# A two-layer decoder trunk on one core: running sums of its own for a shared term of the down product, and other buffers and a priority at the start of the MLP

## The chip, the cores and the metric

The kernel runs on one core of a Trainium2 chip. The metric is the device time of one execution in microseconds (us); lower is better. The engines that matter are TensorE (PE: matmuls, and PEld: its weight loads), VectorE (DVE), ScalarE (ACT), GpSimd (POOL) and SyncE (SP), which here only issues DMAs. Each engine works through its own queue strictly in order: an instruction that waits holds back all that stand behind it.

## The reference, cut to what matters

The trunk has two layers on an activation of 1024 positions by 1024 channels, all float32. Layer 0 mixes tokens with a gated MLP, layer 1 with dilated attention. After each mixer comes the part that the change is about, a dense MLP with squared ReLU:

```python
h = x
for layer in range(DEPTH):                       # DEPTH = 2
    y = _rms_norm(h, mix_norm_g[layer])
    h = h + mixer(y)                             # gMLP, then dilated attention
    y = _rms_norm(h, mlp_norm_g[layer])
    h = h + jnp.square(jax.nn.relu(y @ w_up[layer])) @ w_down[layer]
return _rms_norm(h, final_norm_g)                # D_MODEL 1024, D_FF 4096
```

## The kernel before, in words

**Number format.** Every float32 operand is split into a high and a low part (`split`, L201: ScalarE writes the high part with a copy, L202; VectorE subtracts to get the low part, L203), and every product is three matmul passes (`three`, L327). A tile is 128 partitions by 512 columns; h lies on the chip as eight tiles `h[0..7]` of 128 channels by 1024 positions. `half(s)` is one half of the positions.

**Order.** Only TensorE's order is written out by hand. On the other engines the tile framework orders the instructions ahead of time, by its own estimate of when each will be ready; among instructions that are ready, the one earlier in the program goes first, and `tc.high_priority(offset=PRIO)` moves a group forward by 60 places in that ranking. Buffers come from pools with a fixed number of tiles: `temp()` takes one of eight tiles "t", `spare()` one of two tiles "b", `raw()` one of four tiles "r" (the landing place of weights), `wpair()` one of eight split weight pairs "wp", `pair()` one of 28 larger slots. PSUM has three banks "mm" and five banks "at". Who asks for a tile that is taken waits until its last reader is done.

**The MLP's start** (`mlp`, L647, and `Terms.second`, L402). The up product first runs plainly for two column blocks q = 0 and 1 of the hidden layer. For s = 0, then s = 1, eight groups of twelve matmuls run over four banks; at the end of each s the four banks are evacuated by `squared` (L628: ScalarE Relu from PSUM, L630, and Square in place, L631) into four `temp()` tiles c. With s = 0 three of the banks are mm and one is at; with s = 1 two are at and two are mm, so TensorE needs two mm banks back early in s = 1. While s = 0 runs, `second` makes the normalised input for s = 1: for each k in 0 to 3 two tiles t (L411 and L412, a `temp()` each), their splits, two sums in spares (L416, L417) and two sums on GpSimd (L418, L419). After s = 0 the weights of q = 2 are loaded into raw tiles (`up_weights(2)`, L673).

**The rest of the up product.** For q = 2 to 15 a two-by-two blocking is computed with seven products instead of eight (Winograd's variant of Strassen's scheme); the hidden terms of every q go to DRAM (`hid`).

**The down product** (`Down`, L735). Eighteen steps t = 0 to 17; step t works on the output rows a = t mod 4 and a + 4, and on up to four hidden blocks ks, so the four values of a take turns and each comes four or five times. A full step has seven products of twelve matmuls, in this order: d from w5, b from w6, a_ from w1, e from w7, then d further with w3, a_ further with w2, e further with w4. In between, for the next step: four raw loads of weights and their sums on GpSimd (L357 to L362), seven splits "wp" (`more()`), seven loads t<-hid (`self.inputs`) and their splits "hx". Each product's result is added by VectorE into one of the four blocks `hs[i, s]` of h (`add`, L785, L786). The sum u = b + a_ (M6 + M1) is common to three of the four blocks. Before, every step forms it anew: ScalarE copies a_ to a temp (L803), VectorE adds b (L804), GpSimd adds u to `hs[1,1]`, `hs[1,0]` and `hs[0,1]` (L816, L817). As `a_` takes the w2 product on top, TensorE cannot start it before a_ has been read for u; d with w3 likewise waits until `add(1, 1, d)` (L793) has read d. After the last step `close` (L837) multiplies hidden block 15 in and hands h on to the next norm.

The weights are loaded one step ahead, and the raw tile of a weight is free again when its split is done; SyncE's queue holds the weight loads and the loads t<-hid in one line.

Of the kernel before, what the change touches and what calls it, by code (L numbers as in the profile page):

```python
# [12 lines left out]
AF = mybir.ActivationFunctionType  # L13
# [98 lines left out]
def trunk(ctx: ExitStack, tc: tile.TileContext, xT, w_u, w_v, w_o, w_s, b_s, w_qkv, w_bo, rel,  # L112
# [14 lines left out]
    def temp():  # L127
        return tpool.tile([P, HALF], F32, tag="t", name="t")

    def spare():  # L130
        return tpool.tile([P, HALF], F32, tag="b", name="b", bufs=2)
# [8 lines left out]
    class Pair:  # L140


        def __init__(self, t):
            self.hi, self.lo = t[:, 0, :], t[:, 1, :]
# [15 lines left out]
    def raw():  # L160
        return tpool.tile([P, HALF], F32, tag="r", name="r", bufs=4)
# [218 lines left out]
    class Terms:  # L380
# [21 lines left out]
        def second(self, sq, gi):  # L402
            r = sq.rms()
            yield LAT["rms"]
            pb = spread(r)
            tt = nc.vector.tensor_tensor
            for k in range(4):
                y, x, (y0, y1) = [], [], (self.kept[k][:, j, :] for j in range(2))
                for j in range(2):
                    o = 4 * j + k  # L410
                    t = temp()  # L411
                    nc.vector.scalar_tensor_tensor(t, h[o][:, sq.cols], vec[:, gi, o:o + 1], pb, op0=ALU.mult, op1=ALU.mult)  # L412
                    y.append(t)
                    x.append(pair().split(t))
                t1, t2 = spare(), spare()
                tt(t1, y[0], y0, op=ALU.subtract)  # L416
                tt(t2, y[1], t1, op=ALU.subtract)  # L417
                nc.gpsimd.tensor_tensor(y0, y[1], y[0], op=ALU.subtract)  # L418
                nc.gpsimd.tensor_tensor(y1, y1, t2, op=ALU.subtract)  # L419
                yield 2 * LAT["tile"]  # L420
                for j in range(2):
                    self.blocks[j, 1].append(x[j])
                self.t[5].append(pair("t1").split(t1))
                self.t[6].append(pair("t2").split(t2))
# [203 lines left out]
    def squared(t, src=None):  # L628

        nc.scalar.activation(t, t if src is None else src, AF.Relu)  # L630
        nc.scalar.activation(t, t, AF.Square)  # L631
# [15 lines left out]
    def mlp(layer, x, first, last):  # L647


        def up_weights(q):  # L650
            return Weights(lambda i, j: w_up[layer, q, i, j])


        tiles = [(q, i) for q in range(2) for i in range(2)]
        c = {}
        for s in range(2):
            banks = [at_bank() if (n < 2) == (s == 1) else mm_bank() for n in range(4)]
            if s == 0:
                banks = [mm_bank() if n < 3 else at_bank() for n in range(4)]
            order = [(j, k) for j in range(2) for k in range(4)] if s == 0 else [(j, k) for k in range(4) for j in range(2)]  # L660
            for n, (j, k) in enumerate(order):
                xs = x.blocks[j, s]
                flow.until(lambda: len(xs) > k)
                for b, (q, i) in zip(banks, tiles):
                    three(b, first[q][i, j], blk(k), xs[k], n == 0, n == 7)
                    flow.pump()
            for b, (q, i) in zip(banks, tiles):
                c[q, i, s] = temp()
                squared(c[q, i, s], b)
                if s and i:  # L670
                    hidden_terms(q, c[q, 0, 0], c[q, 1, 0], c[q, 0, 1], c[q, 1, 1], c[q, 0, 0])
            if s == 0:
                w = up_weights(2)  # L673
                for _ in w.steps():
                    pass
        x.rest()

        for q in range(2, 16):
            down = Down(layer) if q == 15 else None
            wn = down.weights(0) if down else up_weights(q + 1)  # L680
            more = ahead(wn)
            more()
            d = at_bank()
            product(d, w[5], x.t[5])
            more()
            c22 = temp()
            nc.scalar.activation(c22, d, AF.Copy)  # L687
            if down:
                down.take(14, held, SEVEN[:4])
            b = at_bank()  # L690
            product(b, w[6], x.t[6])
            more()
            if down:
                down.take(14, held, SEVEN[4:])
            a = mm_bank()
            product(a, w[1], x.t[1])
            more()
            u = temp()
            nc.scalar.activation(u, a, AF.Copy)
            nc.vector.tensor_tensor(u, u, b, op=ALU.add)  # L700
            if down:
                down.early(SEVEN[:4])
            e = at_bank()
            product(e, w[7], x.t[7])
            more()
            nc.vector.tensor_tensor(c22, c22, e, op=ALU.add)  # L706
            nc.vector.tensor_tensor(c22, c22, u, op=ALU.add)
            squared(c22)
            if down:
                down.early(SEVEN[4:])  # L710
            product(d, w[3], x.t[3], True)
            more()
            c12 = temp()
            nc.vector.tensor_tensor(c12, u, d, op=ALU.add)
            squared(c12)
            product(a, w[2], x.t[2], True)
            more()
            c11 = temp()
            squared(c11, a)
            product(e, w[4], x.t[4], True)  # L720
            more()
            c21 = temp()
            nc.vector.tensor_tensor(c21, u, e, op=ALU.add)
            squared(c21)
            if q < 14:
                hidden_terms(q, c11, c21, c12, c22, u)
            elif q == 14:
                held = hidden_terms(q, c11, c21, c12, c22, u, False)
            else:
                kept(q, {(0, 0): c11, (1, 0): c21, (0, 1): c12, (1, 1): c22})  # L730
            w = wn
        down.run(w)
        down.close(last)

    class Down:  # L735


        def __init__(self, layer):
            self.layer = layer
            self.order = [14, *range(14)]  # L740
            self.x = {k: {} for k in self.order}
            self.todo = [(t % 4, range(max(0, t - 3), min(t, 14) + 1)) for t in range(18)]

        def weights(self, t, **kw):
# [28 lines left out]
        def run(self, w):  # L773
            for t, (a, ks) in enumerate(self.todo):
                hs = {(i, s): h[a + 4 * i][:, half(s)] for i in range(2) for s in range(2)}
                wn = None
                if t < 17:
                    wn = self.weights(t + 1, **(dict(own=temp, place=pair) if t == 16 else {}))
                more = ahead(wn)
                more()  # L780

                def xs(p):
                    return [self.x[self.order[k]][p] for k in ks]

                def add(i, s, src, engine=nc.vector):  # L785
                    engine.tensor_tensor(hs[i, s], hs[i, s], src, op=ALU.add)  # L786

                if t == 16:
                    self.ends(0)
                d = at_bank()  # L790
                product(d, w[5], xs(5))
                more()
                add(1, 1, d)  # L793
                self.inputs(t + 1, (5,))
                b = at_bank()
                product(b, w[6], xs(6))
                more()
                self.inputs(t + 1, (6,))
                a_ = mm_bank()
                product(a_, w[1], xs(1))  # L800
                more()
                u = temp()
                nc.scalar.activation(u, a_, AF.Copy)  # L803
                nc.vector.tensor_tensor(u, u, b, op=ALU.add)  # L804
                self.inputs(t + 1, (1,))
                if t == 16:
                    self.ends(1)
                e = at_bank()
                product(e, w[7], xs(7))
                more()  # L810
                add(1, 1, e)
                self.inputs(t + 1, (7,))
                product(d, w[3], xs(3), True)
                more()
                add(0, 1, d)
                for i, s in ((1, 1), (1, 0), (0, 1)):  # L816
                    add(i, s, u, nc.gpsimd)  # L817
                self.inputs(t + 1, (3,))
                product(a_, w[2], xs(2), True)
                more()  # L820
                add(0, 0, a_)
                self.inputs(t + 1, (2,))
                product(e, w[4], xs(4), True)
                more()
                add(1, 0, e)
                self.inputs(t + 1, (4,))
                w = wn

# [554 lines left out]
```

## Time and profile before

| | |
|---|---|
| device time, median of three runs | 2249.78 us (2249.32 to 2254.13) |
| the profiled execution: its own time | 2249.28 us |
| the profiled execution: its span, first to last instruction | 2247.6 us |
| PE busy | 2165.0 us, 96% of the span |
| DVE, ACT, POOL busy | 1605.8, 1096.9 and 636.3 us |
| mean granted TensorE clock | 0.989 |
| matmuls and transposes | 10378 |

The up product with q = 2 and on is at about 340 to 625 us and 1610 to 1898 us, the down product at about 627 to 942 us and 1898 to 2209 us, the attention between the two layers. Where PE never waits, it starts about 222 matmuls in 50 us. A stretch with fewer is a stretch with waits, and only there can the time come down, since the change takes away no matmul. In a row of the timeline stand the start, the duration, the engine, the line, the operation, output<-inputs, the count, and in brackets the idle time before it with what ended it. In the view of waits stand the engine and line that waited, what they waited for, the sum in us, how often, and the longest.

### The profile page before, as it was taken

To read this page: it belongs to the slowest core of one execution; us is meant where nothing else is said; L and a number is where in the kernel's file an instruction comes from. 1 tells how busy PE (TensorE), PEld (TensorE's weight loads), DVE (VectorE), ACT (ScalarE), POOL (GpSimd) and SP (SyncE) were. 2 spreads that over 40 slices of the span, in tenths; PEclk is the share of its full clock that TensorE was granted. 3 is DMA by queue.
4 is the path that set the end of the run, shared out by engine and by line. 5 is a ranking of instruction groups with operands and counts; after the bars stand their busy time and mean duration, and the time that the engine had idled before them with its cause. 6 is when DMAs were issued, how large, how long until landed. Compare 5 with 4: busy or idle time off the path is not lost. (4 is left out here: it accounts for less than half of the span.)

```text
span 2247.6 us, 30296 instructions
## 1 busy us (share of the span) xinstructions
PE 2165.0 (96%) x10378; PEld 1782.2 (79%) x10378; DVE 1605.8 (71%) x2823; ACT 1096.9 (49%) x2253; POOL 636.3 (28%) x456
## 2 busy tenths in 40 slices
PE   8999999999989999999999999999899999999997
PEld 6888877888877777778888888887678888777786
DVE  6875277767798888765664755647887777987877
ACT  6644145555554343456544555646455556444333
POOL 1100223333255555510000000002333333655554
PEclk9999999999999999999999999999999999999998
DMA  6321114444354444301111111120154443444433
GB/s 220 108 76 47 38 41 146 155 155 150 119 167 141 139 138 141 108 30 39 43 40 43 34 40 48 31 52 11 38 182 151 155 155 127 159 141 150 133 102 103
DMA packets 152334, 230.27 MB, mean 102 GB/s; under 512 B 32761, under 2 KB 47220, under 8 KB 152180
## 3 DMA queue, kind: packets, MB, share of 16 engines
q1 hardware_dynamic: 151280, 227.11, 31.5%
q8 instruction: 81, 1.33, 0.2%
q10 hardware_dynamic: 900, 1.23, 0.2%
q14 instruction: 73, 0.60, 0.1%
HBM read 170.45 MB, written 57.84 MB: 102 GB/s over the span
## 5 line engine op out<-in xcount | busy, mean ns | idle before, releaser
L179 PE MATMUL mm<-y,whi 128*128 128x512 f32 x1616 | 508.2, 396 | 1.0 <-DVE h L300 1.0
L179 PE MATMUL at<-hx,wp 128*128 128x512 f32 x1770 | 423.2, 394 | 30.0 <-DVE h L786 25.3
L179 PEld LDWEIGHTS at<-hx,wp 128*128 128x128 f32 x1770 | 333.1, 190 | 109.6 <-ACT wp L202 28.6
L203 DVE TENSOR_TENSOR wp<-r,wp 128x512 fp32r<-128x512 f32 (+3 forms) x388 | 331.3, 862 | 87.7 <-ACT wp L202 86.3
L179 PEld LDWEIGHTS mm<-y,whi 128*128 128x128 f32 x1616 | 296.5, 188 | 62.7 <-DVE h L300 1.4
L202 ACT ACTIVATE wp<-r 128x512 fp32r<-128x512 f32 (+3 forms) x388 | 227.6, 594 | 225.1 <-PE at L179 100.1
L256 POOL TENSOR_TENSOR t<-t 128x512 f32<-128x512 f32 (+1 forms) x66 | 82.7, 1253 | 874.1 <-ACT t L251 862.1
L179 PE MATMUL mm<-y,wlo 128*128 128x512 f32 x808 | 315.8, 391 | 0.0
L179 PE MATMUL at<-t,wp 128*128 128x512 f32 x1344 | 314.4, 390 | 0.1
L179 PEld LDWEIGHTS at<-t,wp 128*128 128x128 f32 x1344 | 252.2, 188 | 53.1 <-DVE t L706 0.9
L202 ACT ACTIVATE hx<-t 128x512 fp32r<-128x512 f32 x192 | 119.1, 626 | 271.0 <-DMA t<-hid 267.5
L203 DVE TENSOR_TENSOR hx<-t,hx 128x512 fp32r<-128x512 f32 x192 | 193.4, 1012 | 73.9 <-ACT hx L202 73.1
L179 PE MATMUL mm<-y,wp 128*128 128x512 f32 x912 | 225.9, 394 | 9.7 <-ACT t L630 9.3
L179 PEld LDWEIGHTS mm<-y,wp 128*128 128x128 f32 x912 | 171.9, 189 | 48.0 <-ACT t L630 10.8
L786 POOL TENSOR_TENSOR h<-h,t 128x512 f32<-128x512 f32 x108 | 164.0, 1535 | 157.7 <-DVE h L786 90.8
L357 POOL TENSOR_TENSOR t<-r 128x512 f32<-128x512 f32 (+3 forms) x62 | 92.4, 1490 | 353.7 <-DMA r<-in_w_up 193.4
L179 PEld LDWEIGHTS mm<-y,wlo 128*128 128x128 f32 x808 | 151.7, 188 | 33.1
L179 PE MATMUL mm<-hx,wp 128*128 128x512 f32 x708 | 172.4, 391 | 4.8 <-ACT t L803 4.8
L203 DVE TENSOR_TENSOR wlo<-r,whi 128x512 fp32r<-128x512 f32 x160 | 111.5, 719 | 74.6 <-ACT whi L202 74.5
L179 PEld LDWEIGHTS mm<-hx,wp 128*128 128x128 f32 x708 | 132.5, 188 | 34.6 <-ACT t L803 7.4
L202 ACT ACTIVATE whi<-r 128x512 fp32r<-128x512 f32 x160 | 97.2, 627 | 116.9 <-PE mm L179 91.2
L179 PE MATMUL at<-y,wp 128*128 128x512 f32 x480 | 120.6, 394 | 3.7 <-ACT t L687 3.0
(191 smaller groups left out, 3117.5 us busy)
## 6 DMA issues: line engine op xcount, KB each, us to landing
t<-hid SPq DMA_DIRECT2D x182, 256.0 KB, 4.0
hid<-t SPq DMA_DIRECT2D x140, 256.0 KB, 2.3
r<-in_w_up SPq DMA_DIRECT2D x128, 256.0 KB, 2.7
r<-in_w_dn SPq DMA_DIRECT2D x88, 256.0 KB, 2.7
r<-in_w_qkv SPq DMA_DIRECT2D x72, 256.0 KB, 2.8
hid<-b SPq DMA_DIRECT2D x56, 256.0 KB, 2.3
r<-in_w_v SPq DMA_DIRECT2D x48, 256.0 KB, 3.5
h<-in_xT SPq DMA_DIRECT2D x16, 256.0 KB, 6.1
```

Of the source, the lines that this page charges most:

```text
L179: nc.tensor.matmul(out, lhsT, rhs, **kw)
L202: nc.scalar.activation(hi, src, AF.Copy)
L203: nc.vector.tensor_tensor(lo, src, hi.bitcast(F32), op=ALU.subtract)
L256: nc.gpsimd.tensor_tensor(self.acc, self.acc, sq, op=ALU.add)
L357: tt(r3, r[0, 0], r[1, 0], op=ALU.subtract)
L786: engine.tensor_tensor(hs[i, s], hs[i, s], src, op=ALU.add)
```

## The change

It has three parts. First, `Terms.second` takes its tiles t from the raw pool instead of the temp pool. Second, the evacuations of the first two column blocks (`squared` after s = 0 and s = 1) get a priority. Third, the down product keeps one sum u per output row group a, `self.u[a]`, over all steps: u[0] and u[1] lie in the two spares, u[2] and u[3] in two temps. In steps 0 to 3 ScalarE copies b into it; from step 4 on VectorE adds b; in every step VectorE adds a_. Only in steps 14 to 17, the last for each a, does GpSimd add it to the three blocks of h; the add to `hs[1, 0]` comes after the add of e.

```diff
@@ Terms.second
-                    t = temp()
+                    t = raw()
@@ mlp
                 c[q, i, s] = temp()
-                squared(c[q, i, s], b)
+                with tc.high_priority(offset=PRIO):
+                    squared(c[q, i, s], b)
@@ Down.__init__
+            self.u = {}
@@ Down.run
                 b = at_bank()
                 product(b, w[6], xs(6))
                 more()
+                if t < 4:
+                    self.u[a] = spare() if t < 2 else temp()
+                    nc.scalar.activation(self.u[a], b, AF.Copy)
+                else:
+                    nc.vector.tensor_tensor(self.u[a], self.u[a], b, op=ALU.add)
                 self.inputs(t + 1, (6,))
                 a_ = mm_bank()
                 product(a_, w[1], xs(1))
                 more()
-                u = temp()
-                nc.scalar.activation(u, a_, AF.Copy)
-                nc.vector.tensor_tensor(u, u, b, op=ALU.add)
+                nc.vector.tensor_tensor(self.u[a], self.u[a], a_, op=ALU.add)
...
                 add(0, 1, d)
-                for i, s in ((1, 1), (1, 0), (0, 1)):
-                    add(i, s, u, nc.gpsimd)
+                if t >= 14:
+                    for i, s in ((1, 1), (0, 1)):
+                        add(i, s, self.u[a], nc.gpsimd)
...
                 add(1, 0, e)
+                if t >= 14:
+                    add(1, 0, self.u[a], nc.gpsimd)
```

## The prediction

> **What bounds the kernel now.** I read the page first (PE busy 96%), then the windows, to see where PE runs short of its own pace, and last who it waits for there.
>
> ```profile
> 400.00:450.00 50.00, 50.00 (x222) 41.41 (x221) 36.70 (x42) 24.82 (x43) 17.34 (x12) 1.00 0.45 156
> 640.00:900.00 260.00, 243.79 (x1050) 197.84 (x1049) 223.84 (x262) 109.07 (x198) 140.51 (x94) 0.99 0.43 142
> 1920.00:2160.00 240.00, 229.58 (x996) 186.26 (x995) 201.44 (x240) 98.43 (x178) 131.11 (x84) 1.00 0.44 144
> 1600.00:1610.00 10.00, 4.14 (x12) 2.67 (x11) 9.89 (x14) 6.27 (x12) 4.43 (x4) 0.72 0.07 26
> ```
>
> The columns are the stretch, its length, busy time and count of PE, PEld, DVE, ACT, POOL, then clock and DMA. The up product (first row) starts 222 matmuls in 50 us, 0.225 us each. At that pace the 1050 and 996 matmuls of the two down stretches would take 236 and 224 us: about 24 and 16 us are lost there. In the ten microseconds of the last row, the MLP's start in layer 1, 12 matmuls start instead of 44. The up product has nothing to give. The waits name the holders:
>
> ```profile
> PE at L179 <- DVE h L786: 27.1, 24, 3.4
> PE mm L179 <- ACT t L630: 9.3, 2, 5.9
> PE mm L179 <- ACT t L803: 4.8, 6, 1.3
> ```
>
> The first and third rows are the down product (adds into h; the copy of a_), the second the MLP's start, once per layer. All three together are 41 us of waiting. The change takes no matmul away, so this is its ceiling.
>
> **The MLP's start.** The timeline of layer 1:
>
> ```profile
> 1598.77 2.20 PE L179 MATMUL at<-y,wp 128*128 128x512 f32 x9
> 1605.68 0.61 ACT L202 ACTIVATE y<-t 128x512 fp32r<-128x512 f32 x1
> 1606.20 0.58 ACT L630 ACTIVATE t<-mm 128x512 f32<-128x512 f32 x1
> 1606.83 3.17 PE L179 MATMUL mm<-y,wp 128*128 128x512 f32 x6 [5.86 <-ACT t L630]
> 333.36 0.63 ACT L202 ACTIVATE y<-t 128x512 fp32r<-128x512 f32 x1 [1.70 <-DVE t L412]
> 333.90 1.06 ACT L630 ACTIVATE t<-mm 128x512 f32<-128x512 f32 x2
> 334.53 2.78 PE L179 MATMUL mm<-y,wp 128*128 128x512 f32 x6 [3.46 <-ACT t L630]
> ```
>
> The nine matmuls are the last three of s = 0 and six of s = 1 on fresh at banks. So the mm banks were complete before 1599, and PE stands at 1600.97 for want of one. ScalarE reaches L630 only at 1606.20, because the split of the last-but-one y stands ahead of it, and that y comes late from VectorE. Layer 0 shows the same order. The priority moves L630 forward, and with the norm's tiles in raw the four c no longer share temps with it. If L630 goes ahead of the y, it ends before or just after PE needs the bank: between nothing and some 1.2 us (two instructions of 0.6) remains per layer. I take 0.6 each: 9.3 less 1.2 is **8 us**. After the long wait the granted clock is 0.72 in that window; I add **1 us** for the clock, an estimate: matmuls at 72% of the pace would lose 0.3 us in each us, for the some three us behind the wait.
>
> The Trainium skill (TensorE: Matmul & The Clock Gate, "Why this matters for your kernels") says that an idle gap of more than about 3 us sends the clock back to half rate. The 0.72 agrees for the gap of 5.86 us; by the rule alone the share for the clock would be between 1 and 2 us.
>
> Of what is late next, I looked at two things. The inputs of s = 1: the last y is split by 1609 (1606.20 + 0.58, one more split of 0.6, then VectorE); PE, unhindered, wants it three groups of 24 matmuls after 1599, at 1615. It stays hidden. The raw tiles:
>
> ```profile
> 1597.27 1.29 POOL L418 TENSOR_TENSOR keep<-t 128x512 f32<-128x512 f32 x1 [4.51 <-DVE b L416]
> 1603.14 0.74 DVE L412 SCALAR_TENSOR_TENSOR t<-h,vec,at 128x512 f32<-128x512 f32 x1
> 1609.28 1.28 POOL L418 TENSOR_TENSOR keep<-t 128x512 f32<-128x512 f32 x1 [2.44 <-DVE b L416]
> 1612.83 1.74 POOL L357 TENSOR_TENSOR t<-r 128x512 f32<-128x512 f32 x1
> 1625.05 2.05 ACT L202 ACTIVATE wp<-r 128x512 fp32r<-128x512 f32 x3 [1.26 <-PE at L179]
> r<-in_w_up SPq DMA_DIRECT2D x128, 256.0 KB, 2.7
> ```
>
> Four raws hold two k at a time; k = 3 (L412 at 1603.14) needs those of k = 1, read for the last time by L418 at 1597.27 to 1598.56, so they are free. But the loads of q = 2's weights, SP's next, now wait for the raws of k = 2 and 3, the last until 1610.56. They land 2.7 us later, at 1613.3, where GpSimd wants them at 1612.83. The weights' splits wait for PE's release of "wp" (1625.05), some 7 us earlier if PE gains. The cover is thin: I charge **+1 us** for both layers, bounds 0 and 4 (a wait of 2 us in each).
>
> **The down product.** One step of the steady part, in order of time:
>
> ```profile
> 769.90 1.68 POOL L786 TENSOR_TENSOR h<-h,t 128x512 f32<-128x512 f32 x1 [3.71 <-DVE h L786]
> 770.34 1.79 DVE L203 TENSOR_TENSOR hx<-t,hx 128x512 fp32r<-128x512 f32 x1
> 772.65 0.68 DVE L203 TENSOR_TENSOR wp<-r,wp 128x512 fp32r<-128x512 f32 x1
> 773.74 0.90 SPq L168 DMA_DIRECT2D t<-hid  x2
> 776.79 0.63 ACT L202 ACTIVATE hx<-t 128x512 fp32r<-128x512 f32 x1 [5.61 <-DMA t<-hid]
> 777.46 1.25 DVE L203 TENSOR_TENSOR hx<-t,hx 128x512 fp32r<-128x512 f32 x1 [1.82 <-ACT hx L202]
> 778.63 0.67 DVE L786 TENSOR_TENSOR h<-h,at 128x512 f32<-128x512 f32 x1
> 779.46 2.97 PE L179 MATMUL at<-hx,wp 128*128 128x512 f32 x12 [0.99 <-DVE h L786]
> 779.83 0.68 DVE L203 TENSOR_TENSOR hx<-t,hx 128x512 fp32r<-128x512 f32 x1
> 780.44 2.38 DVE L203 TENSOR_TENSOR wp<-r,wp 128x512 fp32r<-128x512 f32 x2
> 782.26 2.88 PE L179 MATMUL mm<-hx,wp 128*128 128x512 f32 x12
> 782.28 0.33 SPq L168 DMA_DIRECT2D r<-in_w_dn  x1
> 782.74 0.68 DVE L804 TENSOR_TENSOR t<-t,at 128x512 f32<-128x512 f32 x1
> SPq L168 <- DVE wp L203: 195.2, 40, 7.6
> L804 DVE TENSOR_TENSOR t<-t,at x36: 672/675/690, 632.7 to 2206.2; 128x512 f32<-128x512 f32 x36
> ```
>
> PE's w3 product (779.46) waits 1.0 us for `add(1, 1, d)` (778.63), though d was complete long before. Back from there: that add stands on VectorE behind an hx split, which waits for ScalarE, which waits for a load t<-hid issued at 773.74. SP issued it late because it stands behind a weight load that wants a raw tile, free when VectorE has split w2 (772.65 to 773.33). The SP row shows the rule: 195 of the 260 us of this stretch (640 to 900) SP waits for a wp split. And w2's split is late because an hx split took 1.79 us instead of 0.68 (779.83) while GpSimd added u to h (769.90). The second half of the circle runs from the w5 split (first of the two at 780.44) to the next raw load (782.28) and five more hid loads. **This circle through VectorE, SP and DMA, not PE, sets the step.** Twelve or so such steps per layer wait about 1 us each.
>
> What changes in one step. Removed: one ACT copy (not on the circle) and three POOL adds. The third of these stretched the hx split by 1.79 - 0.68 = 1.1 us, on the circle; the first two fall after 782.74, beside splits that are off it, and count nothing here. Added: VectorE's second add, 0.68 us (the L804 row: 672 to 690 in all 36, also beside GpSimd). It follows the b product, so it falls between the hx split at 779.83 and the two wp splits: ahead of w5, on the circle, +0.68. Kept: the other add, now with a_ instead of b; it no longer waits for the ACT copy and can pass the w6 split. Its wait for PE's w1 product holds the w6 split, `add(1, 1, e)` and the w7 split behind it, all wanted a product or more later. Sum on the circle: -1.1 + 0.7 = -0.4 us a step, 24 steps: **-10 us**. The bounds are +0.3 (both adds ahead of w5: -1.1 + 1.36) and -1.0 (the added one in VectorE's idle 1.8 us at 777.46, and PE at its pace), so +7 and -24 us.
>
> The Trainium skill (SBUF — State Buffer, "Who interferes with whom") has GpSimd and a VectorE instruction with two SBUF inputs exclude each other for a whole instruction, and one with at most one SBUF input not at all. The second half agrees with the L804 row (one input is PSUM). By the first half the split could lose the whole 1.68 us; the trace has 1.1. With 1.68 the sum would be -1.0 a step, -24 us.
>
> Buffers: two temps are now held to the end, u no longer takes one per step. At the burst of five hid loads u and a weight sum took two of eight; now five loads and the weight sum fill six of six. It just fits; an SP order changed by it is in the bounds.
>
> The first steps, with 3 to 9 matmuls per product:
>
> ```profile
> 642.75 1.58 POOL L786 TENSOR_TENSOR h<-h,t 128x512 f32<-128x512 f32 x1
> 643.12 1.62 DVE L203 TENSOR_TENSOR wp<-t,wp 128x384 fp32r<-128x384 f32 x1
> 646.60 8.31 PE L179 MATMUL at<-hx,wp 128*128 128x512 f32 x24 [3.44 <-DVE h L786]
> 632.01 0.96 PE L179 MATMUL mm<-hx,wp 128*128 128x512 f32 x3 [1.31 <-ACT t L803]
> 632.69 0.68 DVE L804 TENSOR_TENSOR t<-t,at 128x512 f32<-128x512 f32 x1
> ```
>
> In both layers PE waits 3.4 us behind VectorE splits, of which GpSimd stretches one by about 1 us: **-2 us**. The six waits for L803 become waits for VectorE's add of a_: as early as PE's end of a_ (-4.8 us), or where L804 stands, 1.4 us past PE's present start, in the two short steps at each end of both layers (+11). I take **0**, as the add no longer needs the copy. The twelve POOL adds per layer that stay lie in the last four steps as before; `add(1, 0, u)`, now last, is due only at the sixth group of `close`, 30 matmuls or 6.8 us on, and takes 1.58 us.
>
> **Sum.** -8 - 1 + 1 - 10 - 2 = -20 us. The profiled execution took 2249.28 us (span 2247.6), 0.5 below the median of 2249.78. So 2229.3 on its own scale, about **2230** on the median's.
>
> **Rivals.** (1) Both adds go ahead of w5: the down product stays as it is, only the start gains: 2241. For it: program order puts them early; against: the a_ add needs the w1 product, after b's. Chance 0.22. (2) The circle falls below PE's pace, as at the lower bound: -24 down, -8 start, -5 first steps and L803: 2212. For it: the waits are only 1.0 us of some 20. Chance 0.15. (3) Slower: the add of a_ now holds PE. The w2 product takes a_ on top and wants it at 782.26; if the add keeps L804's place (end 783.42), PE waits 1.2 us in each of 14 steps per layer, and w2's split, raw and hid loads come that much later: +33 - 8 - 2, 2272. It decides from the point where the add stands behind the w6 split. Against it: the add loses the wait for the copy. Chance 0.14. (4) The start does not do what it says: L630 keeps its place behind y, since that order came from readiness and not from rank: 2238. Chance 0.10. My forecast: 0.39, its own range 2220 to 2238.
>
> **How the numbers follow.** The range leaves out the far half of (3) and the extreme of (2): 2207 to 2258. A measurement can tell about 0.2% from no change. Slower: (3) with a little of (1), 0.15. Same (2245 to 2254): the upper ends of (1) and (4), 0.07. Faster: 0.78.
>
> **What would show it.** Right: the wait for L630 near zero in both layers and L630 ahead of the last two y splits; POOL's L786 24 instead of 108; the hx split before w2 at 0.68 us; the row of waits for L786 well under 27 us; no new row of PE waiting for VectorE's sum above 5 us. Wrong: PE's mm matmuls waiting about 1 us a step for that sum; a q = 2 that waits for its weights; hid loads that come later to SP than before.

## The result and the profile after

| | before | after |
|---|---|---|
| device time, median of 4 runs each | 2251.95 us (2249.32 to 2255.05) | 2203.16 us (2198.97 to 2203.74) |
| ratio, 95% interval | | 0.9779 (0.9759 to 0.9799) |
| profiled execution: own time, span | 2249.28, 2247.6 us | 2202.7, 2201.0 us |

The forecast was 2230, the range 2207 to 2258. The direction was right. The gain, 46.6 us between the two spans, is more than twice the 20 us of the sum, and the time lies 4 us below the range.

TensorE's longest waits in the profile after (engine and line that waited, for whom, us in all, times, longest):

```profile
PE mm L179 <- DVE b L812: 5.0, 5, 1.7
PE at L179 <- ACT t L688: 4.4, 2, 2.7
PE at L179 <- DVE h L791: 4.2, 4, 1.6
PE mm L179 <- DVE t L812: 2.3, 2, 1.2
```

The adds into h (L786 before, L791 now) fell from 27.1 us to 4.2; the 9.3 us for L630 are gone; the 4.8 us for the copy of a_ have become 7.3 us for VectorE's add of a_ (L812). These differences come to 30 us only. Where the 46.6 us came from is better read from TensorE's count of matmuls. In every trace of this case the down product of a layer shows all of its 1260 matmuls on hx tiles: 210 in steps 0 to 3, 840 in steps 4 to 13, 210 in steps 14 to 17. (Steps 3 to 14 are full, with 84 matmuls each; the ten steps 4 to 13 are taken as "the full steps" here.) The windows below run from the first matmul of step 0 to that of step 4, to that of step 14, and to the end of the last one, for both layers; first the kernel before, then the changed one (columns as in the prediction).

```profile
627.14:684.77 57.63, 51.52 (x211) 40.91 (x210) 52.92 (x65) 26.56 (x51) 37.30 (x27) 0.94 0.50 164
684.77:889.23 204.46, 193.05 (x841) 156.97 (x840) 171.56 (x201) 83.08 (x150) 107.17 (x70) 1.00 0.43 142
889.23:942.23 53.00, 50.08 (x212) 40.47 (x211) 41.64 (x64) 21.59 (x45) 26.86 (x25) 0.97 0.35 106
1898.46:1955.52 57.06, 50.98 (x212) 39.96 (x211) 52.83 (x65) 25.95 (x50) 37.61 (x27) 0.97 0.51 164
1955.52:2157.85 202.33, 193.03 (x842) 156.97 (x840) 166.95 (x201) 83.04 (x151) 108.91 (x70) 1.00 0.43 142
2157.85:2208.74 50.89, 48.68 (x212) 39.36 (x211) 41.28 (x61) 17.50 (x38) 25.77 (x24) 1.00 0.26 76
```

```profile
623.89:677.11 53.22, 48.72 (x211) 39.11 (x210) 50.43 (x73) 29.38 (x55) 20.23 (x17) 1.00 0.61 196
677.11:867.51 190.40, 190.40 (x841) 157.71 (x840) 155.96 (x210) 88.44 (x140) 61.45 (x41) 1.00 0.48 150
867.51:917.65 50.14, 48.53 (x212) 39.36 (x211) 35.17 (x60) 16.16 (x35) 22.11 (x22) 1.00 0.33 98
1869.77:1922.96 53.19, 48.72 (x211) 39.11 (x210) 50.32 (x73) 29.35 (x55) 20.59 (x17) 1.00 0.60 196
1922.96:2113.36 190.40, 190.40 (x841) 157.71 (x840) 156.11 (x210) 88.44 (x140) 60.96 (x41) 1.00 0.49 150
2113.36:2162.66 49.30, 48.29 (x212) 39.43 (x211) 34.06 (x57) 13.07 (x29) 23.55 (x22) 1.00 0.21 63
```

The second and fifth row of the second fence are the finding: in both layers the ten full steps take 190.40 us with PE busy for 190.40. That is 19.04 us a step, 0.2267 us a matmul, and PE waits for nothing. Before, a step took 20.3 us (406.8 / 20). From the bounds of these windows and the spans follows the ledger:

| stretch, both layers, in us | forecast | before | after | difference |
|---|---|---|---|---|
| up to step 0, and from the end of step 17 to the next layer's step 0 | -8 | 1583.4 | 1576.0 | -7.4 |
| steps 0 to 3 | -2 | 114.7 | 106.4 | -8.3 |
| steps 4 to 13 | -10 | 406.8 | 380.8 | -26.0 |
| steps 14 to 17 | 0 | 103.9 | 99.4 | -4.5 |
| after the last step | 0 | 38.9 | 38.3 | -0.5 |
| sum | -20 | | | -46.6 |

The forecast's -10 us was for the twelve full steps of each layer, of which the row has ten.

The MLP's start came out as forecast: ScalarE's first two evacuations run at once when the banks are complete, and the third group of matmuls follows without a wait. The timeline of the changed kernel, layer 1:

```profile
1573.09 2.20 PE L179 MATMUL mm<-y,wp 128*128 128x512 f32 x9
1574.12 1.19 ACT L630 ACTIVATE t<-mm 128x512 f32<-128x512 f32 x2
1575.13 2.20 PE L179 MATMUL at<-y,wp 128*128 128x512 f32 x9
1577.17 1.52 PE L179 MATMUL mm<-y,wp 128*128 128x512 f32 x6
```

What the change did to ScalarE, the reader of the loads t<-hid, is seen in its waits between 640 and 880 us, before and after:

```profile
ACT hx L202 <- DMA t<-hid: 128.3, 40, 5.7
```

```profile
ACT wp L202 <- PE at L179: 87.0, 60, 2.2
ACT wp L202 <- PE mm L179: 34.2, 24, 2.2
ACT hx L202 <- DMA t<-hid: 1.2, 2, 0.7
```

Before, ScalarE stood for more than half of this stretch (128 of 240 us) waiting for a load. Now it waits for PE to release a weight pair, which means that it is ahead of PE. The loads arrive before they are needed. Nothing in the prediction said so. Its account of the circle had GpSimd's third add as the cause and the loads as a link that stays.

### The profile page after: what moved, and what is told of

It is laid out like the page before. It is cut to its first block, busy times and chain, and to the rows that moved or that the text cites. A ratio compares the mean times of both kernels' runs of the same rounds, so it can differ in the third digit from the quotient of the medians.

```text
span 2201.0 us, 30298 instructions
## 1 busy us (share of the span) xinstructions
PE 2151.5 (98%) x10378; PEld 1779.2 (81%) x10378; DVE 1563.0 (71%) x2851; ACT 1103.5 (50%) x2225; POOL 503.7 (23%) x372
## 4 chain that ended last, share of the span: by engine, by line
PE 86%; DVE 7%; DMA 2%; ACT 2%; issue 2%; POOL 1%; SPq 0%; DVEq 0%; POOLq 0%; ACTq 0%
PE mm L179 43%; PE at L179 41%; PE at L186 2%; DVE wp L203 1%; DVE y L203 1%; DVE h L791 0%; DVE t L203 0%; ACT t L1044 0%; DMA r<-in_w_v 0%; DVE t L1317 0%; DMA t<-in_w_dl 0%; DVE h L300 0%; DVE b L417 0%; DMA t<-hid 0%; ACT wp L202 0%
## 5 line engine op out<-in xcount | busy, mean ns | idle before, releaser
L179 PE MATMUL at<-hx,wp 128*128 128x512 f32 x1770 | 413.1, 389 | 3.3 <-DVE h L791 3.3
L203 DVE TENSOR_TENSOR hx<-t,hx 128x512 fp32r<-128x512 f32 x192 | 140.2, 733 | 0.5 <-ACT hx L202 0.5
L791 DVE TENSOR_TENSOR h<-h,at 128x512 f32<-128x512 f32 x144 | 97.8, 682 | 56.6 <-PE at L179 56.6
```

The lines of the kernel that those rows point to most:

```text
L179: nc.tensor.matmul(out, lhsT, rhs, **kw)
L203: nc.vector.tensor_tensor(lo, src, hi.bitcast(F32), op=ALU.subtract)
```

## The experiments

Two theories stood at first. **Theory A** is the prediction's: GpSimd's adds stretch VectorE's splits, and that lies on the circle of split, release and load. **Theory B**: u asked for a temp in each step, at a time when PE had just begun the product that u needs; if the tiles of a pool are handed out in the order of the program, the loads of the next step, which ask after u, are planned behind it. With u out of that ring of eight temps they run ahead.

Durations by stage, both layers added, worked out from the same matmul starts in each trace (all 1260 matmuls of each layer are there in each):

| run | u | GpSimd's adds in steps 0 to 13 | steps 0-3 | 4-13 | 14-17 | sum | median us | ratio (95%) |
|---|---|---|---|---|---|---|---|---|
| before | temp per step | yes | 114.7 | 406.8 | 103.9 | 625.4 | 2251.8 | 1 |
| e4_u_in_spares | spare per step | yes | 119.1 | 380.8 | 98.7 | 598.6 | 2223.92 | 0.9873 (0.985 to 0.9896) |
| e9_no_pool_adds | temp per step | none | 106.2 | 390.2 | 102.4 | 598.9 | 2223.52 | 0.988 (0.9864 to 0.9895) |
| e8_dve_adds | temp per step | on VectorE | 112.1 | 387.3 | 103.3 | 602.7 | 2228.81 | 0.9905 (0.9892 to 0.9919) |
| e10_temp_per_step | kept, and a temp per step | none | 106.7 | 383.9 | 106.3 | 596.9 | 2215.98 | 0.9837 (0.9819 to 0.9855) |
| e3_pool_kept | kept | yes | 116.3 | 380.8 | 100.7 | 597.8 | 2210.42 | 0.9823 (0.9807 to 0.9839) |
| e2_down_only | kept | none | 106.7 | 380.8 | 100.4 | 587.9 | 2214.43 | 0.9833 (0.9812 to 0.9853) |
| after | kept | none | 106.4 | 380.8 | 99.4 | 586.6 | 2203.16 | 0.9779 (0.9759 to 0.9799) |

In the column u, "kept" is one sum per row group held over the steps, as in the change. Runs e3, e10 and after have the change's MLP start as well, the others the start of the kernel before; the columns by stage compare them without it. Each ratio is against runs of the kernel before on the same chip, whose medians lie between 2251.5 and 2252.9 us. How far the columns move by themselves is seen in e1, e5 and e6 (below), whose down product is that of the kernel before: 114.5 to 115.1, 406.7 to 411.3 and 102.1 to 102.6.

**u out of the ring, nothing else** (e4, on the kernel before):

```diff
-                u = temp()
+                u = spare()
                 nc.scalar.activation(u, a_, AF.Copy)
```

> The kernel before, with u of each step in one of the two spare tiles instead of a temp; the GpSimd adds, the ScalarE copy and the VectorE add stay in every step. Theory A (the one on record: GpSimd's adds stretch the VectorE splits on the circle): nothing is taken away, so within 4 us of before. Theory B (u's request for a temp stands in the queue for temps ahead of the loads t<-hid and holds them back until PE has finished the a_ product; with u out of that pool the loads run ahead): most of what the down product gained, 25 to 38 us, so 2213 to 2227.

One word of the code gives some 28 us, within theory B's bracket and far outside theory A's. The steps 4 to 13 of layer 0, and ScalarE's wait for the loads in the stretch 640 to 880:

```profile
689.23:879.63 190.40, 190.40 (x841) 157.71 (x840) 176.22 (x203) 92.23 (x150) 114.15 (x71) 1.00 0.46 152
```

```profile
ACT hx L202 <- DMA t<-hid: 4.8, 7, 1.2
```

The full steps are at PE's pace to the hundredth, as in the changed kernel, although every add of GpSimd is still there (114.15 us of work on POOL in that window, against 61.45 after). The wait for the loads is nearly gone. Steps 0 to 3 even lost 4.4 us (119.1 against 114.7).

That the loads are planned otherwise is seen in SyncE's queue. A step has seven loads t<-hid and four of weights (r). One step of the kernel before, then of e4, then of e10, which is told of below:

```profile
773.74 0.90 SPq L168 DMA_DIRECT2D t<-hid  x2
782.28 0.33 SPq L168 DMA_DIRECT2D r<-in_w_dn  x1
782.66 2.33 SPq L168 DMA_DIRECT2D t<-hid  x5
785.09 9.52 SPq L168 DMA_DIRECT2D r<-in_w_dn  x3
```

```profile
781.38 0.42 SPq L168 DMA_DIRECT2D t<-hid  x1
783.90 0.33 SPq L168 DMA_DIRECT2D r<-in_w_dn  x1
784.28 2.80 SPq L168 DMA_DIRECT2D t<-hid  x6
```

```profile
777.86 0.91 SPq L168 DMA_DIRECT2D t<-hid  x2
786.79 0.33 SPq L168 DMA_DIRECT2D r<-in_w_dn  x1
787.17 2.33 SPq L168 DMA_DIRECT2D t<-hid  x5
```

The order with two loads ahead of the single weight load and five behind it stands in all full steps of layer 0 in before, e1, e5, e6, e8, e9 and e10, the runs in which each step asks for a temp besides those for its loads and its weight sum. In e2, e3, e4, e11 and the changed kernel, where it asks for none, it is one and six (in e7, with a temp fewer, the groups lie otherwise again). Matched one by one, a load is issued 4.1 us (median) before ScalarE splits it in the full steps of layer 0 before, 3.9 us in e10, 8.6 us in e4 and 8.9 us in the changed kernel.

**GpSimd's adds away, u still a temp of each step** (e9, on the kernel before):

```diff
-                for i, s in ((1, 1), (1, 0), (0, 1)):
-                    add(i, s, u, nc.gpsimd)
+                if t >= 14:
+                    for i, s in ((1, 1), (1, 0), (0, 1)):
+                        add(i, s, u, nc.gpsimd)
```

> The kernel before, with the three GpSimd adds of u left out in steps 0 to 13 of each down product (u of these steps is formed and not added to h). Theory A: the stretched splits shrink, 1.1 us off each of about 24 steps and 2 us in the first steps, 25 to 30 us less, 2222 to 2227. Theory B: u still takes a temp in every step and the order of loads and splits stays, so the gain is a few us, 2240 to 2250.

The windows of steps 0 to 3 and 4 to 13 in layer 0, and ScalarE's wait for the loads between 640 and 880 us:

```profile
627.17:680.58 53.41, 50.06 (x211) 40.25 (x210) 46.08 (x67) 27.12 (x53) 20.31 (x16) 0.97 0.57 185
680.58:877.09 196.51, 192.32 (x841) 157.14 (x840) 152.65 (x199) 82.46 (x149) 58.81 (x40) 1.00 0.44 144
```

```profile
ACT hx L202 <- DMA t<-hid: 115.2, 39, 5.9
```

The time lies in theory A's bracket and some 16 us below theory B's. So theory A's part is there too: steps 0 to 3 gain all that the change gains in them (106.2 against 106.4), the full steps 0.83 us each (16.6 / 20). But they stay above PE's pace, and ScalarE still waits 115 us for loads.

**The change with GpSimd's adds back** (e3, on the changed kernel):

```diff
-                if t >= 14:
-                    for i, s in ((1, 1), (0, 1)):
-                        add(i, s, self.u[a], nc.gpsimd)
+                for i, s in ((1, 1), (1, 0), (0, 1)):
+                    add(i, s, self.u[a], nc.gpsimd)
...
-                if t >= 14:
-                    add(1, 0, self.u[a], nc.gpsimd)
```

> The changed kernel, but GpSimd adds u to three blocks of h in every step at the old place, so that GpSimd works as much as before (h receives the partial sums several times). Theory A: the contention is back, 1.1 us in each of 24 steps, 2225 to 2232. Theory B: the loads still run ahead and there is slack, 2201 to 2208.

It came 7 us above the changed kernel, just above theory B's bracket and far below theory A's. The window of the full steps in layer 0, and two splits and two adds out of VectorE's timeline there:

```profile
680.81:871.21 190.40, 190.40 (x841) 157.71 (x840) 189.18 (x215) 87.26 (x140) 118.67 (x72) 1.00 0.47 153
```

```profile
752.44 1.78 DVE L203 TENSOR_TENSOR hx<-t,hx 128x512 fp32r<-128x512 f32 x1
754.14 0.68 DVE L791 TENSOR_TENSOR h<-h,at 128x512 f32<-128x512 f32 x1
754.74 0.68 DVE L203 TENSOR_TENSOR wp<-r,wp 128x512 fp32r<-128x512 f32 x1
755.35 1.78 DVE L203 TENSOR_TENSOR hx<-t,hx 128x512 fp32r<-128x512 f32 x1
```

This is the strongest row against the prediction's step. The hx splits shown take 1.78 us, and VectorE is busy for 189.18 of 190.40 us; yet PE never waits. In these steps, with the loads early, a stretched split costs nothing. In steps 0 to 3 GpSimd's adds do cost, 9.9 us (116.3 against 106.4); what makes these steps differ was not tried.

**The added add alone** (e10: as the changed kernel, but each step asks for a temp again where the kernel before does):

```diff
-                nc.vector.tensor_tensor(self.u[a], self.u[a], a_, op=ALU.add)
+                x = temp()
+                nc.scalar.activation(x, a_, AF.Copy)
+                nc.vector.tensor_tensor(self.u[a], self.u[a], x, op=ALU.add)
```

> The kernel before with u summed over the steps as in the change, but a_ is first copied by ScalarE into a temp of its own step, and VectorE adds that copy to u. So GpSimd's adds of u are gone in steps 0 to 13, VectorE has its one more add per step, and each step asks for a temp at the place where the kernel before asks for u's: the order of ScalarE's and SP's instructions in a step is the old one again. It differs from the run without GpSimd's adds (2223.5 us) by the added VectorE add. Theory A (the prediction's: the added add of 0.68 us lies on the circle through VectorE and SP and costs its whole duration): 24 steps by 0.68 us are 16 us, 2238 to 2242 us. Theory B (what the change gains beyond GpSimd's adds comes from the loads that are no longer queued behind u's temp; the added add finds VectorE free): 2222 to 2229 us, and in neither case below 2218 us, since the order is the old one. Should it come to 2213 us or less, the order isn't what gives the rest.

This text calls it the kernel before with u summed; the run was built on the changed kernel and has its MLP start too. So the times expected are some 13 us too high for what was run: less these 13, the 2215.98 us lie at the upper end of theory B's bracket (2209 to 2216) and below theory A's (2225 to 2229). The stages are clearer: against e9 it has one more add per step on VectorE, and its full steps are not 16 us longer but 6 us shorter (383.9 against 390.2). The 0.68 us that the prediction put on the circle cost nothing. Why they are shorter was not tried; adding b early also frees its bank a product earlier. SyncE's order is the old one again (above), and so is ScalarE's wait between 640 and 880 us:

```profile
ACT hx L202 <- DMA t<-hid: 96.7, 42, 6.5
```

The request for a temp brings the late loads back; ScalarE's copy, which comes with it, doesn't do so by itself, since e4 has it too. They cost less here: the full steps are 3.1 us above PE's pace (383.9 against 380.8), in e9 9.4 us.

**All three adds of u on VectorE** (e8, on the kernel before):

```diff
                 for i, s in ((1, 1), (1, 0), (0, 1)):
-                    add(i, s, u, nc.gpsimd)
+                    add(i, s, u)
```

> The kernel before with the three adds of u to the output tiles made by VectorE in place of GpSimd, in every step; nothing else is changed, u stays a temp of its step. VectorE gets 3 more adds of some 0.69 us a step (2.07 us), three times what the change adds, and no split of an hx tile can meet an add on GpSimd. Theory A (the prediction's: VectorE's work lies on the circle of split, release, load, so an add there costs its duration): against the run without GpSimd's adds (2223.5 us) 24 steps by 2.07 us more, 2273 us. Theory B (the circle is closed by the loads, and VectorE has idle time in it that takes the adds, in the window 640 to 880 some 48 us of waits for ScalarE's hx pass): 2222 to 2232 us.

ScalarE's wait for the loads in the same stretch of this run:

```profile
ACT hx L202 <- DMA t<-hid: 93.1, 41, 5.5
```

Theory A's price for an add falls: three adds more in each step on VectorE cost the full steps nothing against e9 (387.3 against 390.2), and 5.9 us in the short first ones. The run is in theory B's bracket, and 0.95% faster than the kernel before, with more adds on VectorE. ScalarE's wait for the loads is still there, 93 us.

**Buffers or their order?** With u elsewhere the loads also have one temp more to themselves (theory D). Two runs take it away again: e11 is e4 with seven temps in the whole kernel, e7 is the changed kernel with u[1] in a temp, which leaves five for the loads instead of six.

```diff
@@ e11, temp()
-        return tpool.tile([P, HALF], F32, tag="t", name="t")
+        return tpool.tile([P, HALF], F32, tag="t", name="t", bufs=7)
@@ e7
-                    self.u[a] = spare() if t < 2 else temp()
+                    self.u[a] = spare() if t < 1 else temp()
```

> The kernel before with u in the spare buffers and GpSimd's adds kept, as in the run that gave 2223.9 us, but with 7 temps in place of 8 in the whole kernel. Theory B (what counts is that no tile other than the loads asks for a temp in a step, so that the loads are planned ahead of their products and the splits of weights and inputs alternate; 7 loads a step need no eighth buffer): 2222 to 2230 us. Theory D (u in the spares gained because the loads got an eighth buffer to themselves): most of the 28 us is given back, 2240 to 2253 us.

> The changed kernel with u of the second output block in a temp instead of a spare buffer, so that the loads of a steady step rotate through 5 temps where the change leaves them 6 (8 less the two that hold u). Theory B: the order stays the changed kernel's, the loads are planned later by one product only: 2202 to 2210 us. Theory D: each buffer taken from the loads costs about as much as the one that u's temp took in the kernel before, 2220 us or more.

e11: 2225.72 us, 0.9877 (0.9861 to 0.9894); e7: 2211.1 us, 0.9818 (0.9803 to 0.9833). The full steps of layer 0 in both, e11 first:

```profile
692.22:882.62 190.40, 190.40 (x842) 157.71 (x841) 174.10 (x203) 92.27 (x150) 115.83 (x71) 1.00 0.47 152
```

```profile
679.01:869.41 190.40, 190.40 (x842) 157.74 (x841) 156.12 (x210) 88.39 (x140) 60.98 (x42) 1.00 0.48 150
```

Theory D falls for the full steps: they stay at 190.40 us with one buffer less, in either. The comparison with e10 says the same from the other side: e10 leaves six temps to the loads, the weight sum and its extra tile, and ScalarE waits 96.7 us for loads; e7 leaves five and ScalarE waits 3.9 us. e7 came 1 us above theory B's bracket. Its cost in the down product is nearly all in steps 14 to 17 (110.2 against 99.4 in both layers). There PE waits 4.3 us in layer 0 and 3.9 us in layer 1 for splits of the last step's weights, which are loaded into temps, so there the depth of the ring counts.

**The MLP's start.** e1 is both of its edits on the kernel before, e5 the raw tiles alone, e6 the priority alone, e2 the down product without the start:

```diff
@@ e1, e5
-                    t = temp()
+                    t = raw()
@@ e1, e6
-                squared(c[q, i, s], b)
+                with tc.high_priority(offset=PRIO):
+                    squared(c[q, i, s], b)
```

> The kernel before with only the two edits at the MLP's start (norm tiles in raw buffers, priority for the evacuations). Both theories of the down product say the same here: the positions of equal matmuls in the two traces lie 5.2 us (layer 0) and 5.1 us (layer 1) further apart after the start than before it, so about 10 us less than the kernel before, 2241 to 2243, ratio 0.9955. If the start did more, or the down product draws on it, it is below 2238.

> The kernel before with the raw buffers for the MLP's input tiles alone, no priority. Theory C1 (the temps that the evacuations of the first four tiles get were held by the input tiles, so the buffers are what frees them): 2238 to 2242 us, as the start's two edits together (2238.6). Theory C2 (ScalarE's place for the evacuations is what matters, the buffers only let the priority be kept): 2248 to 2252 us.

> The kernel before with the priority of the first evacuations alone, input tiles in temps as before. Theory C1 (the temps are what is missing): 2248 to 2252 us, no change. Theory C2 (the priority is what matters): 2238 to 2242 us.

> The change's down product alone, without the MLP start's other buffers and priority. If the two parts add up, it is the changed kernel's 2203.2 us plus the 13.2 us that the start alone gave: 2214 to 2218 us. If part of what the start gives in the changed kernel comes from the way that the first down product leaves the queues (the loss in TensorE's waits at the second layer's start is 5 us in the changed kernel as in the first), it is 2208 to 2213 us.

e1: 2238.57 us, 0.9946 (0.9926 to 0.9966), 2.4 us below its bracket. e5: 2243.37 us, 0.9955 (0.9938 to 0.9972), 1.4 us above theory C1's bracket and 4.6 below theory C2's. e6: 2252.88 us, 1.0 (0.9988 to 1.0013), 0.9 us above theory C1's. e2: 2214.43 us, which is the changed kernel's 2203.2 and the 13.2 of e1 but for 2 us: the two parts add up. In e6 the wait is still there:

```profile
PE mm L179 <- ACT t L630: 8.8, 2, 5.4
```

In e5 there is no such row. So the priority by itself gains nothing, as theory C1 has it, and the raw tiles are what takes the wait away. What the priority adds to them (2243.4 to 2238.6) lies within the two intervals and stays open.

**Can more be had?** In the changed kernel PE still waits 7.3 us for L812, 4.2 for L791 and 4.4 for L688. v1 gives priority to the add of a_; v2 also to the adds into h and to the copy in L688; r_after is the changed kernel again on the same chip.

```diff
@@ v1, v2
-                nc.vector.tensor_tensor(self.u[a], self.u[a], a_, op=ALU.add)
+                with tc.high_priority(offset=PRIO):
+                    nc.vector.tensor_tensor(self.u[a], self.u[a], a_, op=ALU.add)
@@ v2
-                    engine.tensor_tensor(hs[i, s], hs[i, s], src, op=ALU.add)
+                    with tc.high_priority(offset=PRIO):
+                        engine.tensor_tensor(hs[i, s], hs[i, s], src, op=ALU.add)
...
-            nc.scalar.activation(c22, d, AF.Copy)
+            with tc.high_priority(offset=PRIO):
+                nc.scalar.activation(c22, d, AF.Copy)
```

> The changed kernel with priority for VectorE's add of a_ to u (line 812), so that it doesn't queue behind splits of weights in the short first and last steps, where TensorE waits for it 7.3 us in all. If these waits are what they seem: 2196 to 2199 us. If the splits that it passes are then late for the next product: 2201 to 2205 us.

> As the run before this one, and priority also for VectorE's adds of the products to the output tiles (line 791, 4.2 us of TensorE's waits) and for ScalarE's copy at the head of each round of the MLP (line 688, 4.4 us). If all three waits go and nothing else gets late: 2189 to 2194 us. If moving the adds of the output tiles ahead in every step makes the splits late: 2203 us or more.

> The changed kernel again, beside the other three on the same chip, so that they can be compared: 2199 to 2206 us.

v1 2203.27 us (2197.16 to 2206.68), v2 2205.09 us (2203.98 to 2213.2), r_after 2205.29 us (2204.12 to 2205.35). Neither can be told from the changed kernel, which is the second case of either expectation. TensorE's waits in v1:

```profile
PE at L179 <- DVE h L791: 7.3, 6, 1.5
PE mm L179 <- DVE b L813: 4.2, 4, 1.7
```

The waits for the add of a_ went down from 7.3 to 4.2 us (L813 here), those for the adds into h went up from 4.2 to 7.3. The priority changed who is waited for.

## Why the prediction was right or wrong

**The circle as the bound: right, but its cause was half of it.** That SP, VectorE and the loads set the step and not PE was borne out: full steps run at PE's pace as soon as the loads come early (e4). Of two things that delayed the loads only one was seen. Each alone gives some 27 us in the down product (625.4 to 598.6 and 598.9), both together 38.8. They are less than additive because the full steps end at PE's pace: u out of the ring reaches it alone, so there GpSimd's adds have nothing more to give.

**-10 us for the full steps: the term that failed.** It was -1.1 for the stretched split and +0.68 for the added add, over 24 steps. The first was measured as -0.83 in each of the 20 full steps (e9). The second is wrong: e10 and e8 show adds on VectorE in these steps without a cost. VectorE has idle time within the circle, before the change in front of the very hx splits that wait for ScalarE. The prediction had that row (1.82 us idle at 777.46) and used it for its lower bound only. And the release of the loads, -26.0 us by itself (e4), is missing: this is the step that failed. A smaller point of reading: the stretch of 1.1 us is nearly all that the exclusion weighed in the prediction allows. The split (770.34) began 0.44 us after GpSimd's add (769.90 to 771.58) and ended 0.55 us after it, less than the 0.68 us that it takes alone; so it hardly advanced beside the add.

**"It just fits; an SP order changed by it is in the bounds."** This is the sentence in which the largest cause was passed over. The temps were counted, eight wanted and eight there, as if a ring that suffices could cost nothing. What counted was that a late request stood in it ahead of the loads (e4), while a buffer less does no harm in the full steps (e11, e7). That the loads are then planned earlier is seen in SyncE's rows and in ScalarE's waits, 128.3 us before, 96.7 in e10, 4.8 in e4, 1.2 after; an order written out by hand, with u still in the ring, was not tried.

**-2 us for steps 0 to 3: mis-sized, -8.3.** The place and the cause were right (e9 has all of it). The step counted the stretch of one split of 1 us per layer. What the wait of 3.44 us in each layer set off was left out. From the kernel before, the 24 matmuls behind it in layer 0 and 1 (the first of them is in the prediction), and the clock granted meanwhile:

```profile
1917.26 7.37 PE L179 MATMUL at<-hx,wp 128*128 128x512 f32 x24 [3.44 <-DVE h L786]
```

```profile
646.60:655.00 8.40, 8.40 (x26) 6.75 (x27) 8.40 (x10) 1.90 (x3) 5.94 (x4) 0.67 0.50 166
1918.00:1926.00 8.00, 8.00 (x29) 6.39 (x29) 8.00 (x9) 1.90 (x3) 5.49 (x4) 0.79 0.48 150
```

At 0.2267 us a matmul these 24 take 5.4 us; they took 8.3 and 7.4. So each of the two waits cost 2 to 3 us more than its 3.4, and the changed kernel's longest wait in steps 0 to 3 is 1.7 us with a clock of 1.00. The rule of the Trainium skill (TensorE: Matmul & The Clock Gate, "Why this matters for your kernels"), by which a gap of more than about 3 us drops the clock, was weighed at the MLP's start and not applied here, where the trace agrees with it as well.

**0 for the waits of the last steps: -4.5 measured.** e4 has that too (98.7); e9 has not (102.4, where e1, e5 and e6 with the old down product have 102.1 to 102.6), which points to u's temp again. No input loads are left in these steps, but the last step's weights land in temps (e7); what u's temp held up was not traced. The waits for L812 (7.3 us) replaced those for L803 (4.8) as the bounds allowed.

**-8 for the start: right** (-7.4 in the ledger; e1, which has the start alone, has -9.2 in the same two stretches of its trace, and -13.2 by the medians, with an interval from 7.7 to 16.7). The waits of 9.3 us went whole. The wait for the copy at the head of a round grew from 3.0 to 4.4 us, which looks like the charge of 1 us for late weights, but is another chain: in both kernels that copy stands in ScalarE's queue behind a weight split that waits 2.7 to 2.8 us for GpSimd's sum. What rival 4 said of the priority holds for the priority alone (e6); the raw tiles carried the gain.

**The ceiling of 41 us: wrong.** The sum of three rows of waits is no ceiling. The gain was 46.6 us, with 11.5 us of such waits left. Rows of waits leave out the smaller holders and the slow matmuls behind a wait. A count at pace was at hand: 2520 matmuls by the 0.225 us of the prediction's first row are 567 us, of 625.4.

**Which case came.** Rival 2, the circle below PE's pace, with a chance of 0.15: -24 down, -8 start, -5 first steps and L803, 2212. Measured were -26, -7.4 and -12.8. Rivals 1 and 3 had the adds on VectorE delay w5 or PE in every full step; 190.40 of 190.40 us rules both out. Of the signs named, L630 before the last two y, GpSimd's 24 adds into h in place of 108, and hx splits near their undisturbed time (733 ns in the mean, 1012 before) all came. The rows, the last of them before and the others after:

```profile
L791 POOL TENSOR_TENSOR h<-h,t 128x512 f32<-128x512 f32 x12 | 17.2, 1436 | 31.3 <-DVE h L791 28.6 <-DMA r<-in_w_qkv 2.6
L791 POOL TENSOR_TENSOR h<-h,b 128x512 f32<-128x512 f32 x12 | 16.2, 1368 | 10.0 <-DVE h L791 9.9
L203 DVE TENSOR_TENSOR hx<-t,hx 128x512 fp32r<-128x512 f32 x192 | 140.2, 733 | 0.5 <-ACT hx L202 0.5
L203 DVE TENSOR_TENSOR hx<-t,hx 128x512 fp32r<-128x512 f32 x192 | 193.4, 1012 | 73.9 <-ACT hx L202 73.1
```

VectorE's idle time before hx splits went from 73.9 to 0.5 us, since their loads come early. That, and not the 733 ns, goes with the steps at pace: e3 has them with splits of 1.78 us.

## What to carry to other kernels

A tile that is asked for late in each step should not share a ring of buffers with the loads of the next step: count not only how many tiles fit, but which request stands ahead of which, and give the late one a pool of its own. Work out what can be gained from the count of matmuls at full pace, stage by stage, not from the sum of the waits. Read the order of a DMA queue in two runs side by side; here it tells the runs with late loads from the others. Where two causes delay the same loads, take each away alone before pricing it; the second is worth only what the first leaves above the pace.

## What the hardware showed unexpectedly

VectorE can be busy for 99.4% of a stretch (189.18 of 190.40 us in e3) with hx splits stretched to 1.78 us, and TensorE still does not wait once, in a run whose loads come early. The adds with one PSUM input stayed at 0.67 to 0.69 us in the same stretch, also where they ran beside an instruction of GpSimd. And a wait of 3.44 us cost TensorE 5 to 6 us, because the 24 matmuls behind it ran at a granted clock of 0.67 (layer 0) and 0.79 (layer 1).
